# Retention of the first four heads moved beside the gate and query products of the last four

## The chip, the core and the metric

One core of a Trainium2 chip runs the whole program. The metric is the device time of one execution in microseconds (us); the median of three runs of the kernel before is 1373.83 us. All tensors in memory are float32. Where a product is written as three TensorE instructions (`mm3`), each factor has been split beforehand into a rounded part and a remainder of type fp32r ("high" and "low").

## What is computed

The reference is one layer of a hybrid network over 1024 tokens of width 1024, with 256 context tokens. Cut to what matters here:

```
hx  = modulate(rmsnorm(x), c);  ux = hx @ w_in            # 3584 columns
x0, x1, v = short_conv(ux[:, :1536])                      # three groups of 512
y_hy  = (long_conv(v * x1, filter) + bias * v * x1) * x0  # through a Fourier transform
q, k, v, g = ux[:, 1536:]                                 # 8 heads x 64 each
q, k  = rope(q), rope(k / 8)
o     = chunkwise retention forward + backward            # chunks of 128 tokens, state from context
y_ret = groupnorm(o) * gn * silu(g)
x     = x + gate1 * (concat(y_hy, y_ret) @ w_out)
x     = x + gate2 * (relu(modulate(rmsnorm(x)) @ w1)**2 @ w2);  out = rmsnorm(x)
```

`modulation()` makes the shift, scale and gate vectors: products of c with slices of w_ada, summed on VectorE (DVE).

## The kernel before, in words

The order in which work is traced gives each instruction a priority; a scheduler at build time then fixes one order for each engine by those priorities and its own estimate of when operands are ready. At run time each engine and each DMA queue goes through its list in order. `urgent()` raises the priority of what stands in it. The stages are:

1. Start (to about 54 us): norms, the filter network, the first two modulation vectors.
2. Key stage (54 to 260 us). The spectra of the filter are made (`pkf`), and for each half `hh` of the heads (four each) the keys (`pk`), values (`pv`) and their context forms (`pck`, `pcv`). Rotated keys `kr` (one buffer) are transposed (`pkT`) and weighted (`kw`, L779) for the chunk states (`pT`). The modulation vectors come in eight pieces of 512 columns. A piece is eight loads `adaw` (three buffers), eight DVE instructions into `adac` (L710, L712) and eight small matmuls `pada` (L715). Pieces 1 to 3 are traced in this stage, behind the value products.
3. Convolution (260 to about 520 us). For each half `hv` of the channels come the products x1, v and x0, features on partitions (`feature_major`: 96 matmuls of 512 columns for a slab of 256 features), the forward transforms `pXv`, the inverse `pGv`, butterflies on DVE, and a last multiplication by x0 (`vxl`) into `mix_d`. Pieces 4 and 5 of the modulation lie here.
4. Gates and queries (431 to 556 us), four slabs with tokens on partitions (`token_major`: 192 matmuls of 256 columns for a slab). Gates go through Silu; queries are rotated on DVE, written twice side by side (`q2`) and stored. Pieces 6 to 8 lie here.
5. Retention (556 to 672 us), 16 chunks, beside eight blocks `poh` of the output projection's convolution half (192 matmuls of 512 columns). A chunk loads its tiles, transposes the doubled queries (`pqd`), weights them (`qw`), copies them into zero-padded tiles (`sgqz`), forms the scores `psc` against the keys (two matmuls of 128 rows and 256 columns), masks them (`sT`) and forms `po` in 64-row halves.
6. The retention half of the projection (`por`), the second norm, and the two MLP products in Strassen form, to the end. Nothing here is changed.

A weight slab is loaded in two halves through one raw buffer `wr`, cast on ScalarE (ACT) and its remainder subtracted on DVE (`slab`, L205 to L207); two slabs are held at a time.

Of the kernel before, what the change touches and what calls it, by code (L numbers as in the profile page):

```python
# [17 lines left out]
P = 128  # L18
D = 1024
# [25 lines left out]
def shape_constants():  # L45
# [48 lines left out]
    rc = np.repeat(cs, 2, axis=1)  # L94
    rs = np.stack([-sn, sn], axis=-1).reshape(T, HD)
# [10 lines left out]
def lay_out(inputs):  # L106
# [3 lines left out]
    a = {n: k[n] for n in ("dft_f", "dft_i", "rope", "posd", "posr")}  # L110
# [20 lines left out]
    a["w_in"] = v["w_in"][0].reshape(KC, P, -1, 256).transpose(2, 1, 0, 3)  # L131
# [9 lines left out]
def tile_hymba_block(ctx: ExitStack, tc: tile.TileContext, I: dict, out: bass.AP, dbg=None, stop=99):  # L141
# [71 lines left out]
    for hv in range(2):  # L213
        cols += [("x1", hv, X1C + 256 * hv), ("vh", hv, VHC + 256 * hv), ("x0", hv, X0C + 256 * hv)]
    cols += [("g", 0, GC), ("g", 1, GC + 256), ("q", 0, QC), ("q", 1, QC + 256)]
# [350 lines left out]
    def rope(dst, ps, tab, n0, pool, nm, twice=None, tag="rope2", bufs=1):  # L566
# [4 lines left out]
        t2 = pool.tile([P, n, 256], F32, tag=tag, bufs=bufs, name=f"rp{nm}{n0}")  # L571
        for j in range(n):
            V.tensor_tensor(t2[:, j].rearrange("p (h i s) -> p h i s", h=4, s=2),
                            ps[:, j].rearrange("p (h i s) -> p h i s", h=4, s=2)[:, :, :, ::-1],
                            bc(tab[:, 1, n0 + j].rearrange("p (i s) -> p i s", s=2), 1, [P, 4, 32, 2]), op=ALU.mult)
        if twice is None:
            V.tensor_tensor(dst, dst, t2, op=ALU.add)
        else:
            V.tensor_tensor(twice, bc(dst.rearrange("p n (h d) -> p (n h) d", h=4), 2, [P, 4 * n, 2, HD]),
                            bc(t2.rearrange("p n (h d) -> p (n h) d", h=4), 2, [P, 4 * n, 2, HD]), op=ALU.add)  # L580
# [161 lines left out]
    for hh in range(2):  # L742
        hs = slice(4 * hh, 4 * hh + 4)
        kr = kvp.tile([P, NCH, 256], F32, tag="kr", name=f"kr{hh}")
# [55 lines left out]
        modulation()  # L800
        if hh == 1:
            modulation()
# [38 lines left out]
    for hv in range(2):  # L841
        vT = vtp.tile([P, NCH, 256], F32, tag="vT", name=f"vT{hv}")
        Gs = cvp.tile([P, 2, 8, 256], F32, tag="Gs", name=f"Gs{hv}")
# [6 lines left out]
        for b, ps in feature_major(("vh", hv), f"pvh{hv}"):  # L850
# [7 lines left out]
            for q in range(2):  # L858
# [3 lines left out]
                A.copy(vT[:, 4 * q:4 * q + 4, b * P:(b + 1) * P], pt.rearrange("p (c n) -> p c n", n=P))  # L862
        for b, ps in feature_major(("x0", hv), f"px0{hv}"):
# [4 lines left out]
            if b == 0:  # L868
                prefetch()
        modulation()  # L870
        prefetch()
        for r, u in butterflies(cvp, scp, vT, 256, f"v{hv}"):
# [88 lines left out]
        for ca, cb, ya, yb, sg in ((C16, S16, 1, 7, 1), (S16, C16, 3, 5, -1)):  # L961
# [7 lines left out]
            tt(Y[yb], z, sub, Y[yb])  # L969
        for b in range(2):  # L970
            blk = 2 * hv + b
            yv = yy[:, b].rearrange("p c n -> p (c n)")
            for q in range(2):
                cc = slice(q * 512, q * 512 + 512)
                vx = cvp.tile([P, 512], F32, tag="fx", bufs=2, name=f"vxl{blk}{q}")
# [7 lines left out]
                dbg(f"mix{blk}_{q}", vx)  # L983
    if stop <= 3:
        return


    sg_d = [tc.dram_tile([2, P, 1024], F32, name=f"sg_d{hh}") for hh in range(2)]
    q2_d = [tc.dram_tile([NCH, P, 8 * HD], F32, name=f"q2_d{hh}") for hh in range(2)]
    for hh in range(2):  # L990
        for g, ps in token_major(("g", hh), f"pgt{hh}"):
            sg = scp.tile([P, 4, 256], F32, tag="sc", bufs=3, name=f"sg{hh}{g}")
            with urgent():
                A.activation(sg, ps, AF.Silu)
                SP.dma_start(sg_d[hh][g], sg.rearrange("p n d -> p (n d)"))
            if hh + g < 2:
                modulation()
        prefetch()
    for hh in range(2):
        for g, ps in token_major(("q", hh), f"pq{hh}"):  # L1000
            with urgent():
                for m in range(2):
                    n0 = 4 * g + 2 * m

                    q2 = scp.tile([P, 2, 4, 2, HD], F32, tag="sc", bufs=3, name=f"q2{hh}{n0}")
                    qr = scp.tile([P, 2, 256], F32, tag="bfs", bufs=2, name=f"qr{hh}{n0}")
                    rope(qr, ps[:, 2 * m:2 * m + 2], ropes, n0, scp, f"q{hh}",
                         twice=q2.rearrange("p j h r d -> p (j h) r d"), tag="bfs", bufs=2)
                    SP.dma_start(q2_d[hh][n0:n0 + 2].rearrange("j p n -> p j n"),
                                 q2.rearrange("p j h r d -> p j (h r d)"))  # L1010
        if hh == 0:
            prefetch()
    cpool("cvp")
# [5 lines left out]

# [10 lines left out]
    rtl = opool("rtl", side="right")  # L1030
    rtp = opool("rtp", side="right")
# [3 lines left out]
    tabq = place(10, "tabq", F32)  # L1035
    SP.dma_start(tabq.rearrange("p a n -> p (a n)"), tab_d.rearrange("p a h n -> p (a h n)"))
    wqT, msk = [tabq[:, 2 * i:2 * i + 2].rearrange("p a (h n) -> p (a h) n", n=P) for i in range(2)]

    mx = [[place(2 * h + i, f"mx{h}{i}") for i in range(2)] for h in range(2)]
    ctrs = place(11, "ctrs", F32).rearrange("p a n -> p (a n)").rearrange("p (b j n) -> p b j n", b=2, j=4)  # L1040
    sgqz = place(12, "sgqz", F32)
    sg = sgqz[:, 0:2].rearrange("p a n -> p (a n)").rearrange("p (j n) -> p j n", j=4)
    mraw = place(13, "mraw", F32)


    qz = [sgqz[:, 2 + i].rearrange("p (h n) -> p h n", h=4) for i in range(2)]
    with urgent():
        for t in qz:
            V.memset(t, 0.0)
# [24 lines left out]
    def retention(hh, n, ctr, gss):  # L1074
        hs = slice(4 * hh, 4 * hh + 4)
        j = n % 4
        nm = f"{hh}_{n}"
        q2 = rtl.tile([P, 4, 2 * HD], F32, tag="q2", bufs=2, name=f"q2l{nm}")
        SP.dma_start(q2.rearrange("p h d -> p (h d)"), q2_d[hh][n])
        kt = rtl.tile([P, 2, P], F32, tag="ktl", bufs=2, name=f"ktl{nm}")  # L1080
        SP.dma_start(kt.rearrange("p a n -> p (a n)"), kT_d[hh][n])
        vt = rtl.tile([P, 256], F32, tag="vtl", bufs=2, name=f"vtl{nm}")
        SP.dma_start(vt, v_d[hh][n])
        st = rtl.tile([P, 256], F32, tag="stl", bufs=2, name=f"stl{nm}")
        SP.dma_start(st[0:64], st_d[hh][0, n])
        SP.dma_start(st[64:128], st_d[hh][1, 7 - n])
# [3 lines left out]
        pqv = pq.rearrange("p (h c) -> p h c", h=4)  # L1090
        qw = rtp.tile([P, 4, P], F32, tag="qw", bufs=2, name=f"qw{nm}")
        V.tensor_tensor(qw, pqv, wqT[:, hs], op=ALU.mult)
        qT = qz[n % 2]
        A.copy(qT[0:64, 0:4:2], pqv[0:64, 0:4:2])
        A.copy(qT[64:128, 1:4:2], pqv[64:128, 1:4:2])
        pc = ps_aux(f"psc{nm}")
        for pr in range(2):
            PE.matmul(pc[:, pr * 256:(pr + 1) * 256], lhsT=kt[:, pr],
                      rhs=qT[:, 2 * pr:2 * pr + 2].rearrange("p h c -> p (h c)"), start=True, stop=True)
        sT = rtp.tile([P, 4, P], F32, tag="sT", bufs=2, name=f"sT{nm}")  # L1100
        V.tensor_tensor(sT, pc.rearrange("p (h c) -> p h c", h=4), msk[:, hs], op=ALU.mult)
        po = ps_cv(f"po{nm}")
        for h in range(4):
            cc = slice(h * HD, (h + 1) * HD)
            for w, o, first in ((sT, vt, True), (qw, st, False)):
                for r in range(2):
                    rows = slice(64 * r, 64 * r + 64)
                    PE.matmul(po[rows, cc], lhsT=w[:, h, rows], rhs=o[:, cc], start=first, stop=not first)
        pov = po[:, 0:256].rearrange("p (h d) -> p h d", h=4)
        mu = rtp.tile([P, 4], F32, tag="mu", bufs=2, name=f"mu{nm}")  # L1110
        V.tensor_reduce(mu, pov, axis=AX.X, op=ALU.add)
        V.scalar_tensor_tensor(ctr[:, j].rearrange("p (h d) -> p h d", h=4), bc(mu, 2, [P, 4, HD]), -1.0 / HD, pov,
                               op0=ALU.mult, op1=ALU.add)
        sq = rtp.tile([P, 256], F32, tag="sqo", name=f"sqo{nm}")
# [482 lines left out]
```

## Time and profile before

| | |
|---|---|
| median of three runs | 1373.83 us (1373.09 to 1375.27) |
| profiled execution, its own time | 1370.97 us |
| span of its profile | 1369.2 us |
| TensorE (PE) matmuls busy | 1294.8 us, 95% of the span |
| DVE busy | 973.3 us, 71% |
| ACT busy | 533.6 us, 39% |
| mean granted TensorE clock | 0.980 |

The span is the time from the first to the last profiled instruction; the execution's own time is 1.8 us longer. A matmul's busy time overlaps its neighbours', so what a matmul costs is read from the distance between two starts.

### The profile page before, as it was taken

What the parts mean: (1) busy time and instruction counts of PE and PEld (TensorE: products, weight loads), DVE (VectorE), ACT (ScalarE), POOL (GpSimd) and SP (SyncE); (2) the same over time, 40 slices, a digit from 0 to 9 for tenths busy, and PEclk for the clock granted to TensorE, in tenths of its full rate; (3) what the DMA queues carried; (4) which work ended last, traced back from release to release, by engine and by line L of the source; (5) the groups of instructions that cost most, each with busy time, mean ns of one, the idle gap of its engine ahead of it and who ended that gap; (6) DMA issues with size and microseconds to landing.
All of it is one profiled execution on the core that took longest, in us unless ns stands there. A gap on an engine that the chain in (4) does not pass through costs nothing.

```text
span 1369.2 us, 20105 instructions
## 1 busy us (share of the span) xinstructions
PE 1294.8 (95%) x7386; PEld 1083.1 (79%) x7386; DVE 973.3 (71%) x1721; ACT 533.6 (39%) x912; POOL 19.4 (1%) x24
## 2 busy tenths in 40 slices
PE   6899899999999999799896999999998999999996
PEld 1479798988788999678776888888886888888896
DVE  5889787357878775558887988888656945555563
ACT  6863432213133121223455444444445744344420
POOL 0140000000000000000000000000000000000000
PEclk9799999999999999999998999999999999999999
DMA  9445766273536644776321789988636996666621
GB/s 374 175 151 160 233 206 212 79 228 129 169 120 215 206 162 155 270 243 182 104 96 64 251 306 326 348 302 300 238 123 232 338 321 190 193 201 185 199 79 62
DMA packets 139570, 278.19 MB, mean 203 GB/s; under 512 B 14672, under 2 KB 47056, under 8 KB 137040
## 3 DMA queue, kind: packets, MB, share of 16 engines
q1 hardware_dynamic: 137744, 272.19, 59.5%
q0 software_dynamic: 1152, 4.19, 0.8%
q8 instruction: 58, 0.95, 0.3%
q10 hardware_dynamic: 576, 0.52, 0.1%
q14 instruction: 40, 0.33, 0.1%
HBM read 193.75 MB, written 83.10 MB: 202 GB/s over the span
## 4 chain that ended last, share of the span: by engine, by line
PE 77%; DVE 8%; DMA 7%; ACT 4%; issue 2%; SPq 1%; POOL 0%; DVEq 0%; ACTq 0%; POOLq 0%
PE px L184 6%; PE px L185 6%; PE px L183 6%; PE pw L183 5%; PE py L183 5%; PE py L185 5%; PE py L184 5%; PE pw L185 5%; PE pw L184 5%; DMA dft_f_k<-in_dft_f 2%; PE pga L397 1%; PE pq L185 1%; PE pq L184 1%; PE pq L183 1%; PE pGv L901 1%
## 5 line engine op out<-in xcount | busy, mean ns | idle before, releaser
L1191 DVE TENSOR_TENSOR mt<-tr,mt 128x512 fp32r<-128x512 f32 x112 | 76.6, 688 | 99.6 <-ACT mt L1190 99.4
L1190 ACT CAST mt<-tr 128x512 fp32r<-128x512 f32 x112 | 69.6, 621 | 123.5 <-PE py L185 67.1
L183 PE MATMUL px<-mt,mw 128*128 128x512 f32 (+1 forms) x320 | 112.5, 352 | 3.0 <-ACT mw L1190 2.4
L184 PE MATMUL px<-mt,mw 128*128 128x512 f32 (+1 forms) x320 | 112.5, 352 | 0.7 <-DVE mt L1191 0.7
L185 PE MATMUL px<-mt,mw 128*128 128x512 f32 (+1 forms) x320 | 111.6, 350 | 0.0
L1191 DVE TENSOR_TENSOR mw<-wr,mw 128x512 fp32r<-128x512 f32 x112 | 76.6, 686 | 4.8 <-ACT mw L1190 4.4
L183 PE MATMUL py<-mt,mw 128*128 128x512 f32 x192 | 74.7, 389 | 0.0
L184 PE MATMUL py<-mt,mw 128*128 128x512 f32 x192 | 74.7, 389 | 0.0
L185 PE MATMUL py<-mt,mw 128*128 128x512 f32 x192 | 74.7, 389 | 0.0
L1190 ACT CAST mw<-wr 128x512 fp32r<-128x512 f32 x112 | 69.0, 617 | 9.8 <-DMA wr<-in_w_mlp 5.5
L183 PEld LDWEIGHTS px<-mt,mw 128*128 128x128 f32 x320 | 61.1, 191 | 11.4 <-ACT mw L1190 2.8
L184 PEld LDWEIGHTS px<-mt,mw 128*128 128x128 f32 x320 | 61.1, 191 | 9.2 <-DVE mt L1191 1.2
L185 PEld LDWEIGHTS px<-mt,mw 128*128 128x128 f32 x320 | 60.9, 191 | 8.2 <-DVE mw L1191 0.3
L183 PE MATMUL px<-hxh,wh_x 128*128 128x512 f32 x128 | 50.7, 396 | 0.0
L184 PE MATMUL px<-hxl,wh_x 128*128 128x512 f32 x128 | 50.6, 395 | 0.0
L185 PE MATMUL px<-hxh,wl_x 128*128 128x512 f32 x128 | 50.6, 395 | 0.0
L712 DVE SCALAR_TENSOR_TENSOR adac<-adaw,cs,adac 128x512 f32<-128x512 f32 x56 | 42.9, 766 | 9.8 <-DMA adaw<-in_w_ada 9.2
L185 PE MATMUL pk<-wh_k,hxl 128*128 128x256 f32 x128 | 39.2, 307 | 3.3 <-DVE hxl L438 3.3
L184 PEld LDWEIGHTS py<-mt,mw 128*128 128x128 f32 x192 | 36.0, 188 | 7.5
L183 PEld LDWEIGHTS py<-mt,mw 128*128 128x128 f32 x192 | 36.0, 188 | 7.5
L185 PEld LDWEIGHTS py<-mt,mw 128*128 128x128 f32 x192 | 36.0, 188 | 7.4
L183 PE MATMUL pk<-wh_k,hxh 128*128 128x256 f32 x128 | 39.6, 310 | 0.4 <-ACT hxh L434 0.4
(500 smaller groups left out, 3764.0 us busy)
## 6 DMA issues: line engine op xcount, KB each, us to landing
tr<-t_d SPq DMA_DIRECT2D x112, 256.0 KB, 4.0
adaw<-in_w_ada SPq DMA_DIRECT2D x64, 256.0 KB, 4.0
WH<-in_w_mlp SPq DMA_DIRECT2D x16, 1024.0 KB, 7.4
s_d<-WH SPq DMA_DIRECT2D x16, 1024.0 KB, 5.0
wr<-s_d SPq DMA_DIRECT2D x64, 256.0 KB, 4.0
wr<-in_w_mlp SPq DMA_DIRECT2D x48, 256.0 KB, 4.2
t_d<-c SPq DMA_DIRECT2D x40, 256.0 KB, 4.1
t_d<-CH SPq DMA_DIRECT2D x40, 256.0 KB, 5.4
```

What stands on the lines that cost most here:

```text
L183: PE.matmul(o, lhsT=lh, rhs=rh, start=first, stop=False, **kw)
L184: PE.matmul(o, lhsT=lh, rhs=rl, start=False, stop=False, **kw)
L185: PE.matmul(o, lhsT=ll, rhs=rh, start=False, stop=last, **kw)
L397: PE.matmul(pga[h][0:4, n, :], lhsT=cv[:, k, :], rhs=w_[:, n * 512:(n + 1) * 512], start=(k == 0), stop=(k == KC - 1 and i == 1))
L712: V.scalar_tensor_tensor(ac, wa, cs[:, k, 0:1], ac, op0=ALU.mult, op1=ALU.add)
L901: PE.matmul(o, lhsT=y[:, 0, cb], rhs=iv[:, sl[0]], start=True, stop=False)
L1190: A.copy(hi, src)
L1191: V.tensor_tensor(lo, src, hi.bitcast(F32), op=ALU.subtract)
```

## The change

Gates and queries become feature-major like the convolution's products. The columns of q and k in w_in are permuted on the host, so that the two members of a rotated pair lie 32 apart. The queries' partners are fetched by four transfers of 32 partitions within SBUF and multiplied with a table `ropeT` (`rot`). A chunk loads its queries already transposed, twice (64 partitions each), so that `pqd`, the doubled store and the zero-padded copies go. The scores become four matmuls of 64 rows and 128 columns, alternating between the lower and the upper 64 partitions, into two PSUM tiles. The retention of heads 0 to 3 runs in memory that the convolution leaves, beside the products of q and g of heads 4 to 7 (`gate_query(1)`); heads 4 to 7 run beside all eight blocks `poh`. Gated results of the first heads go through DRAM (`y_d`). The x0 slabs follow both halves' x1 and v. All eight modulation pieces are traced ahead of the key products, four for each half. From the seventh slab on, raw weights are loaded from POOL's queue.

```diff
@@ slab
-            SP.dma_start(raw, src[:, ks])
+            (SP if nxt[0] < 6 else G).dma_start(raw, src[:, ks])
@@ key stage
     for hh in range(2):
+        for _ in range(4):
+            modulation()
         kr = kvp.tile([P, NCH, 256], F32, tag="kr", name=f"kr{hh}")
...
         prefetch()
-        modulation()
-        if hh == 1:
-            modulation()
@@ convolution
-                vx = cvp.tile([P, 512], F32, tag="fx", bufs=2, name=f"vxl{blk}{q}")
+                vx = cvp.tile([P, 512], F32, tag="bfy", bufs=2, name=f"vxl{blk}{q}")
...
+    yy0 = conv_dft(0, conv_in(0))
+    vT1 = conv_in(1)
+    conv_gate(0)
+    with urgent():
+        conv_out(0, yy0)
+    conv_gate(1)
+    yy1 = conv_dft(1, vT1)
+    with urgent():
+        conv_out(1, yy1)
@@ gates and queries
-        for g, ps in token_major(("g", hh), f"pgt{hh}"):
...
-        for g, ps in token_major(("q", hh), f"pq{hh}"):
...
+    def gate_query(hh):
+        for b, ps in feature_major(("q", hh), f"pq{hh}"):
             with urgent():
+                qf = scp.tile([P, T], F32, tag="sc", bufs=3, name=f"qf{hh}{b}")
+                A.copy(qf, ps)
+                qs = scp.tile([P, T], F32, tag="sc", bufs=3, name=f"qs{hh}{b}")
+                for i in range(4):
+                    SP.dma_start(qs[32 * i:32 * i + 32], qf[32 * (i ^ 1):32 * (i ^ 1) + 32])
+                V.tensor_tensor(qs, qs, rot[:, 1], op=ALU.mult)
+                V.tensor_tensor(qf, qf, rot[:, 0], op=ALU.mult)
+                V.tensor_tensor(qf, qf, qs, op=ALU.add)
+                SP.dma_start(q_d[hh][b * P:(b + 1) * P], qf)
+            yield
+        prefetch()
+        for b, ps in feature_major(("g", hh), f"pgt{hh}"):
+            with urgent():
+                sg = scp.tile([P, T], F32, tag="sc", bufs=3, name=f"sg{hh}{b}")
                 A.activation(sg, ps, AF.Silu)
+                SP.dma_start(sg_d[2 * hh + b], sg)
+            yield
         prefetch()
+    for _ in gate_query(0):
+        pass
@@ retention
-        q2 = rtl.tile([P, 4, 2 * HD], F32, tag="q2", bufs=2, name=f"q2l{nm}")
-        SP.dma_start(q2.rearrange("p h d -> p (h d)"), q2_d[hh][n])
+        q2 = rtl.tile([P, 4, P], F32, tag="q2", bufs=2, name=f"q2l{nm}")
+        for r in range(2):
+            SP.dma_start(q2[64 * r:64 * r + 64], q_d[hh].rearrange("(h d) t -> d h t", h=4)[:, :, n * P:(n + 1) * P])
...
-        pq = ps_aux(f"pqd{nm}")
-        for h in range(4):
-            PE.transpose(pq[:, h * P:(h + 1) * P], q2[:, h], ident)
...
+        pc = [ps_aux(f"psc{nm}{s}") for s in range(2)]
         for pr in range(2):
-            PE.matmul(pc[:, pr * 256:(pr + 1) * 256], lhsT=kt[:, pr],
-                      rhs=qT[:, 2 * pr:2 * pr + 2].rearrange("p h c -> p (h c)"), start=True, stop=True)
+            for s in range(2):
+                rows = slice(64 * s, 64 * s + 64)
+                PE.matmul(pc[s][:, pr * P:(pr + 1) * P], lhsT=kt[rows, pr], rhs=q2[rows, 2 * pr + s],
+                          start=True, stop=True)
...
+    opool("gap", side="right").tile([P, 4 * 1024], F32, name="gap")
+    open_retention()
+    retention_tables(lambda nm: rt["l" if nm == "tabq" else "p"].tile([P, 4, 512], F32, name=f"{nm}0"))
+    products = gate_query(1)
+    def last_heads(g, j):
+        if j % 2:
+            next(products)
...
+    heads(0, last_heads)
+    cpool("rtp")
...
+    def projection(g, j):
+        if j % 2:
+            out_conv(4 * g + 2 * (j // 2))
+            out_conv(4 * g + 2 * (j // 2) + 1)
...
+        if (g, j) in ((0, 2), (1, 0)):
+            for i in range(2):
+                raw = mraw[:, 2 * (j // 2) + i]
+                SP.dma_start(raw, y_d[i][g])
+                split_ret(g, i, raw)
+    wo = []
+    heads(1, projection)
```

## Rows read from the trace of the kernel before

**Rows 1.** Stretch, length, busy us (count) of PE, PEld, DVE, ACT, POOL; clock; DMA.
```profile
54.00:205.00 151.00, 139.04 (x1022) 123.07 (x1022) 126.82 (x300) 74.17 (x148) 16.32 (x16) 0.95 0.60 188
205.00:240.00 35.00, 31.78 (x274) 29.30 (x273) 27.48 (x53) 9.94 (x21) 0.00 (x0) 1.00 0.71 212
240.00:260.00 20.00, 20.00 (x200) 18.68 (x200) 1.29 (x2) 4.31 (x11) 0.00 (x0) 1.00 0.10 36
260.00:555.60 295.60, 290.11 (x1695) 257.60 (x1693) 214.14 (x396) 65.07 (x87) 0.00 (x0) 1.00 0.53 175
555.60:570.00 14.40, 7.08 (x20) 4.77 (x19) 10.06 (x16) 4.52 (x7) 0.00 (x0) 0.76 0.68 219
570.00:672.00 102.00, 98.54 (x896) 77.85 (x897) 73.97 (x135) 32.28 (x71) 0.00 (x0) 1.00 0.63 203
```

**Rows 2.** Timeline of PE (start, us, engine, line): value products of the convolution, first and last of a stretch.
```profile
284.30 0.39 PE L183 MATMUL pvh<-hxh,wh_vh 128*128 128x512 f32 x1
...
297.90 0.39 PE L183 MATMUL pvh<-hxh,wh_vh 128*128 128x512 f32 x1
```

**Rows 3.** The query products' tile: count, shortest/median/longest ns, first and last start.
```profile
L183 PE MATMUL pq<-wh_q,hxh x128: 283/283/283, 509.4 to 555.1; 128*128 128x256 f32 x128
```

**Rows 4.** Timeline of PE in the retention stage: a group of each kind and its neighbours.
```profile
626.95 1.03 PE L1098 MATMUL psc<-sgqz,ktl 128*128 128x256 f32 x4
627.82 0.60 PE L1089 MATMUL pqd<-cols,q2l 128*128 128x128 f32 x4
628.17 0.48 PE L185 MATMUL poh<-mx,wl_o 128*128 128x512 f32 x1
628.49 0.39 PE L183 MATMUL poh<-mx,wh_o 128*128 128x512 f32 x1
628.81 0.34 PE L1108 MATMUL po<-vtl,sT 128*64 128x64 f32 x4
...
629.89 0.50 PE L184 MATMUL poh<-mx,wh_o 128*128 128x512 f32 x1
```

**Rows 5.** Timeline of all engines at the handover from queries to projection; brackets: idle before.
```profile
557.28 0.50 PE L183 MATMUL poh<-mx,wh_o 128*128 128x512 f32 x1 [1.66 <-ACT mx L1057]
...
560.53 0.59 PE L183 MATMUL poh<-mx,wh_o 128*128 128x512 f32 x1 [2.74 <-DVE rpq L573]
...
563.30 0.79 PE L184 MATMUL poh<-mx,wh_o 128*128 128x512 f32 x1 [2.19 <-DVE mx L1058]
```

**Rows 6.** Waits from 260 to 672 us: who waited for whom, us, times, longest.
```profile
PE pada L715 <- DVE adac L712: 2.0, 2, 1.1
PE pqd L1089 <- DMA q2l<-q_d: 1.7, 1, 1.7
PE psc L1098 <- ACT sgqz L1095: 1.6, 2, 0.9
```

**Rows 7.** DVE instructions by line and form: busy us, mean ns, idle before.
```profile
L712 DVE SCALAR_TENSOR_TENSOR adac<-adaw,cs,adac 128x512 f32<-128x512 f32 x56 | 42.9, 766 | 9.8 <-DMA adaw<-in_w_ada 9.2
L579 DVE TENSOR_TENSOR q<-qr,rpq 128x1024 f32<-128x1024 f32 x8 | 9.7, 1215 | 0.2
L573 DVE TENSOR_TENSOR rpq<-pq,ropes 128x256 f32<-128x256 f32 x16 | 6.0, 413 | 0.0
```

**Rows 8.** DVE's time in the modulation sums, key stage and behind it.
```profile
54.00:260.00 206.00, 12.40 (x16) 0.96 0.57 177
260.00:509.00 249.00, 34.29 (x48) 1.00 0.54 173
```

**Rows 9.** DMA issues by line: count, KB, median us to landing.
```profile
eo_d<-eo POOLq DMA_DIRECT2D x8, 512.0 KB, 4.4
wr_g<-in_w_in SPq DMA_DIRECT2D x4, 512.0 KB, 4.7
```

**Rows 10.** SP's queue: the second half's last two stores of the convolution's result.
```profile
514.28 0.32 SPq L982 DMA_DIRECT2D mix_d<-vxl  x1
...
522.01 0.32 SPq L982 DMA_DIRECT2D mix_d<-vxl  x1
```

More of the change, by code (lines that the diff above doesn't have):

```diff
@@ L129, in lay_out @@
     a["w_ada"] = v["w_ada"][0]
-    a["w_in"] = v["w_in"][0].reshape(KC, P, -1, 256).transpose(2, 1, 0, 3)
+    w = v["w_in"][0].copy()
+    for c0 in (QC, KCOL):
+        w[:, c0:c0 + 512] = w[:, c0:c0 + 512].reshape(D, NH, 32, 2).transpose(0, 1, 3, 2).reshape(D, 512)
+    a["w_in"] = w.reshape(KC, P, -1, 256).transpose(2, 1, 0, 3)
     a["w_out"] = v["w_out"][0].reshape(2, 4, P, 2, 512).transpose(0, 3, 2, 1, 4).reshape(4, P, 4, 512)
@@ L839, in short_conv, with conv_in @@
                                op0=ALU.mult, op1=ALU.add)
-    for hv in range(2):
+    def conv_in(hv):
         vT = vtp.tile([P, NCH, 256], F32, tag="vT", name=f"vT{hv}")
-        Gs = cvp.tile([P, 2, 8, 256], F32, tag="Gs", name=f"Gs{hv}")
         x1t = []
@@ L1013, in tile_hymba_block, with open_retention, retention_tables @@
-    cpool("cvp")
+    for _ in gate_query(0):
+        pass
+    rt = {}
+    def open_retention():
+        rt["l"] = opool("rtl", side="right")
+        rt["p"] = opool("rtp", side="right")
+    def retention_tables(new):
+        ctrs, sgs, tabq = [new(nm) for nm in ("ctrs", "sgs", "tabq")]
+        SP.dma_start(tabq.rearrange("p a n -> p (a n)"), tab_d.rearrange("p a h n -> p (a h n)"))
+        rt["wqT"], rt["msk"] = [tabq[:, 2 * i:2 * i + 2].rearrange("p a (h n) -> p (a h) n", n=P) for i in range(2)]
+        rt["ctr"] = ctrs.rearrange("p a n -> p (a n)").rearrange("p (b j n) -> p b j n", b=2, j=4)
+        rt["sg"] = sgs
@@ new lines, in group_norm @@
+    def group_norm(hh, g, sg, ctr, gss):
+        rtp = rt["p"]
+        gv = gss.rearrange("p n h -> p (n h)")
+        V.tensor_scalar(gv, gv, 1.0 / HD, EPS, op0=ALU.mult, op1=ALU.add)
+        rso = rtp.tile([P, 16], F32, tag="rso", bufs=2, name=f"rso{hh}{g}")
+        rsqrt_small(rso, gv, 16, rtp, f"o{hh}{g}")
+        zv = ctr.rearrange("p n (h d) -> p (n h) d", h=4)
+        V.tensor_tensor(zv, zv, bc(rso, 2, [P, 16, HD]), op=ALU.mult)
+        for pr in range(2):
+            pt = ps_cv(f"pz{hh}{g}{pr}")
+            for j in range(4):
+                PE.transpose(pt[:, j * P:(j + 1) * P], ctr[:, j, pr * P:(pr + 1) * P], ident)
+            blk = 2 * hh + pr
+            gn = colsA[:, GN + blk:GN + blk + 1]
+            V.scalar_tensor_tensor(sg[:, pr], pt, gn, sg[:, pr], op0=ALU.mult, op1=ALU.mult)
+            if hh == 0:
+                SP.dma_start(y_d[pr][g], sg[:, pr])
+            else:
+                split_ret(g, blk, sg[:, pr])
@@ new lines, in heads @@
+    def heads(hh, more):
+        pending = None
+        for g in range(2):
+            ctr = rt["ctr"][:, g]
+            gss = rt["p"].tile([P, 4, 4], F32, tag="gss", bufs=2, name=f"gss{hh}{g}")
+            for j in range(4):
+                retention(hh, 4 * g + j, ctr, gss)
+                if j == 1 and pending:
+                    group_norm(*pending)
+                if j == 1:
+                    sg = rt["sg"][:, 2 * g:2 * g + 2]
+                    for pr in range(2):
+                        SP.dma_start(sg[:, pr], sg_d[2 * hh + pr][:, 512 * g:512 * g + 512])
+                more(g, j)
+            pending = hh, g, sg, ctr, gss
+        group_norm(*pending)
@@ L1014, in tile_hymba_block @@
+    opool("gap", side="right").tile([P, 4 * 1024], F32, name="gap")
[5 more added lines that the diff above has]
+            next(products)
+        if (g, j) == (1, 3):
+            next(products, None)
+    heads(0, last_heads)
+    cpool("rtp")
+    cpool("rtl")
+    cpool("gap")
     cpool("vtp")
@@ L1072, in out_conv @@
             slabs.pop(("o", d // 4))
[L1074 to L1077, printed above, removed]
-        q2 = rtl.tile([P, 4, 2 * HD], F32, tag="q2", bufs=2, name=f"q2l{nm}")
-        SP.dma_start(q2.rearrange("p h d -> p (h d)"), q2_d[hh][n])
[L1080 to L1086, printed above, removed]
-        pq = ps_aux(f"pqd{nm}")
-        for h in range(4):
-            PE.transpose(pq[:, h * P:(h + 1) * P], q2[:, h], ident)
[L1090 to L1097, printed above, removed]
-            PE.matmul(pc[:, pr * 256:(pr + 1) * 256], lhsT=kt[:, pr],
-                      rhs=qT[:, 2 * pr:2 * pr + 2].rearrange("p h c -> p (h c)"), start=True, stop=True)
[L1100 to L1114, printed above, removed]
-        A.activation(sq, ctr[:, j], AF.Square)
-        V.tensor_reduce(gss[:, j], sq.rearrange("p (h d) -> p h d", h=4), axis=AX.X, op=ALU.add)
@@ L1164, in tile_hymba_block @@
-    group_norm(*pending)
+    for d in range(KC):
+        SP.dma_start(xn[d], I["xT"][d * P:(d + 1) * P])
+    def projection(g, j):
+        if j % 2:
+            out_conv(4 * g + 2 * (j // 2))
+            out_conv(4 * g + 2 * (j // 2) + 1)
+        if (g, j) == (0, 1):
+            wo.append(slab(I["w_out"][2], "o2", o2))
+        if (g, j) == (0, 3):
+            wo.append(wpool.tile([P, 4, 512], F32, tag="wh", bufs=2, name="o3r"))
+            SP.dma_start(wo[1], I["w_out"][3])
+        if (g, j) in ((0, 2), (1, 0)):
[3 more added lines that the diff above has]
+                split_ret(g, i, raw)
@@ L1165, in tile_hymba_block @@
+    wo = []
+    heads(1, projection)
+    o3r = wo.pop()
     with urgent():
```

159 lines of the change are left out of this document (69 added, 90 removed).

## Prediction

> **What bounds the kernel now.** I read the busy time by stretch first. From 260 to 555.6 us PE is busy 290.1 of 295.6 us and from 570 to 672 us 98.5 of 102, while DVE has 214.1 and 74.0 [rows 1]. The reader should see that TensorE's own work sets the time of the convolution, of the gate and query products and of the retention. A reordering there gains nothing by itself: it must remove PE work or PE's holes. Three places differ. In the key stage PE lacks 15.2 us (139.0, 31.8 and 20.0 of 206) and DVE is busy 155.6 us; 18.7 of its 50.4 idle us lie in the last 20 us, where PE is full [rows 1]. Second, the 14.4 us from 555.6 hold 20 matmuls and a clock of 0.76 [rows 1]. Third, the retention pays for small fp32 matmuls between the large ones.
>
> Since busy times overlap, I took prices from the distance of starts in PE's timeline. The convolution's products start 60 matmuls in 297.90 - 284.30 = 13.60 us, 0.227 us each for 512 columns [rows 2]. Query products start 127 triples in 45.7 us, 0.120 us each for 256 columns [rows 3]. Then I read the handover, the waits and the lines of DVE [rows 5 to 8].
>
> The sum is made against the profiled execution, 1370.97 us (span 1369.2 and 1.8 around it). The median of the runs shown, 1373.83, is 2.9 us above it; I add the sum's difference to the median. A difference under 0.2%, 2.7 us, can hardly be told from none.
>
> **1. Gates and queries feature-major.** A slab is 192 x 0.120 = 23.0 us now and 96 x 0.227 = 21.8 after [rows 2, 3]. Four slabs: -5.0 us, within half a microsecond, as both forms run in this trace. The queries' rotation becomes three DVE passes of 1024 columns for each of four half slabs, about 1.2 us a pass (the form of L579 [rows 7]), 15 us in all, behind an ACT copy and a transfer of partners. It is hidden by the next half slab's 48 x 0.227 = 10.9 us, as PSUM holds two. Uncovered, it would cost the last block's chain once, some 10 us, but the last blocks are gates, which need one ACT pass.
>
> **2. Transposes of the queries go.** Four `pqd` take 628.17 - 627.82 = 0.35 to 0.36 us, 16 chunks: -5.8 us [rows 4]. ACT's zero-padded copies go too; they ended two holes of PE, 1.6 us [rows 6], counted in 5.
>
> **3. Scores.** Four instructions of 256 columns take 627.82 - 626.95 = 0.87 us [rows 4]. After there are eight of 128 columns (two passes for each of four matmuls), on alternating halves of the rows. The trace shows no pairs of row halves. Upper bound: each costs half of one now, 0.11 us, plus 0.1 us at both ends, as a large matmul beside a `po` group takes 0.32 instead of 0.227 us [rows 4]: 1.08 us, +3.4 us for 16 chunks. Lower bound: they overlap as the `po` groups do, which use column halves: 32 of 64 columns in 629.89 - 628.81 = 1.08 us, 0.034 each [rows 4]; at 128 columns 0.067, 0.54 us a chunk, -5.3 us. `po` is the nearest kin, so I take its rate with both ends paid, 0.74 us: -2 us.
>
> The boundary of 0.1 us above is a row. The Trainium skill (TensorEngine Tiling (Array Packing), Key Properties) has a rule on each side: tiles of a split array work in parallel, and a change of the tiling mode drains the engine. By the first alone the scores would save 0.43 us a chunk, about 7 us; by the drain without overlap they would lose the 3.4 us. No trace so far shows such pairs of row halves.
>
> **4. The handover.** In the 14.4 us behind the last query product, 20 matmuls at 0.227 need 4.5 us: 9.9 us are lost, through a cast (1.66), DVE's rotation of the last queries (2.74), the remainder of the mixed block (2.19) and the low clock, 0.76, after those holes [rows 1, 5]. After, the same handover stands behind the last gate product, since the split convolution result still takes the memory of `hx`. DVE's rotation is gone from it, and raw blocks can be loaded ahead. I take half, -5 us; bounds 0 and, if only the first cast is left, -8.2.
>
> **5. Other holes from 260 to 672 us.** PE lacks 5.5 us up to 555.6 and 3.5 after 570 [rows 1]; the waits on `pada`, on the queries' load and on the copies are 5.3 of them [rows 6]. I take -2.5; bounds 0 and -5.3. The first heads' retention needs PE about 8 x 1.8 us plus transposes, 16 us, beside two slabs, 43.5 us; the second heads the same beside 192 x 0.227 = 43.6. Each chunk has four small DVE passes and one more of 0.41 us (the mask in two halves, L573's form [rows 7]); DVE has 28 us free there [rows 1]. So retention lies beside other work as before, and only its place changes.
>
> **6. Modulation in the key stage.** Of 64 sums, 46.7 us, 16 run there now; 48 more are 34.3 us for DVE [rows 8]. Its queue would be busy 189.9 of 206 us. Behind an `adac` stand the rotation of the keys, `kw` and the transforms' sums; PE waits for those. What hides them is DVE's idle time, 50.4 us, and that PE has the next products. Lower bound nothing: the weights `kw` are late by less than the 21.8 us of the next slab. Upper bound: the 18.7 us at the end help nobody, the idle rest is used only to half, so 34.3 - 16 = 18 us reach PE, and six more `pada` groups wait 1.1 us each as the longest now [rows 6]: 25 us. Where 48 sums lie today, PE waited 2.0 us on them [rows 6], with DVE idle 28% of the time against 24% in the key stage [rows 1]; I take +4, nearer to that row. Their loads matter less: DVE idled 9.2 us on them in the whole run [rows 7].
>
> **7. Edits costed at nothing.** Twenty-two half slabs move to POOL's queue. A store there lands in 4.4 us, a slab half on SP's in 4.7 [rows 9]; two halves with a cast and a remainder of some 1.2 us each (L579's form) take 14 us of a slab's 21.8, so 7 us more would be needed before PE sees it. SP gains free slots and gives them to 16 partner transfers, one more query load a chunk and four `y_d` stores. The x0 slabs only change places among equal matmuls. `vx` in its own buffers shortens the last multiplication, whose stores are now 7.7 us apart [rows 10].
>
> Sum: -5.0 - 5.8 - 2 - 5 - 2.5 + 4 = -16.3 us, 1354.7 for the profiled execution and 1357.5 for the median. All bounds low: -5 - 5.8 - 5.3 - 8.2 - 5.3 = -29.6, 1344. All high: -5 - 5.8 + 3.4 + 25 = +17.6, 1391.
>
> **The rivals.**
> *A. DVE becomes the bound of the key stage (slower).* Place: 54 to 240 us, where DVE already has 154.3 of 186 us [rows 1]. For it: 34 us are put where 31.7 are idle, and `kr` has one buffer, so the second half's rotation waits for the first half's `kw`. Against it: PE can take the values' or x1's products meanwhile. Price: term 6 at its upper bound, -20.3 + 25 = +4.7, 1378.5. It decides from 23 us on.
> *B. The cover comes late.* The first heads' memory is free only when the second half's convolution has stored its result. Now that is 33 us before the last query product [rows 3, 10], so of the x0 slab and four others behind the second value slab, 21.8 + 92 = 114 us, some 80 pass beside it; after there are two x0, a q and a g slab, 87 us: a margin of 7 us. If it is 20 us late, PE takes the last heads' products ahead, a retention without cover idles about half of that, and the handover keeps its price: -16.3 + 10 + 5, near 1372.5. Against it: three pieces of modulation leave DVE's queue there, and the stores come closer together.
> *C. Row halves don't overlap.* The scores cost +3.4 instead of -2: 1363. [...]
> *D. Nothing is lost.* Terms 3 to 5 near their low bounds and term 6 near nothing: 1346.
>
> **How the numbers follow.** Forecast (1351 to 1361): 0.42. C (1361 to 1366): 0.13. B (1366 to 1376.5): 0.15. A (above 1376.5): 0.17. D (below 1351): 0.13. Time 1358, that of the likeliest. The range from 1346 to 1379 leaves out the lower half of D and two thirds of A, under 0.2; the likeliest case's own range is 1351 to 1361. Faster by over 0.2% is below 1371.1: forecast, C, D and a little under half of B, 0.74. Same, 1371.1 to 1376.6: 0.09. Slower: A, 0.17.
>
> **What would show it.** Right: gate and query matmuls of 512 columns start 0.227 us apart; no `pqd`; PE fuller than 95% from the first gate product to `por`; `por` begins some 15 to 20 us earlier, the later stages moved but not changed. Term 6: PE's idle time from 54 us to the first x1 product against 15.2 us, and DVE's share there. Term 3: time from a score group's first start to the next group. Term 4: idle and clock behind the last gate product. The prediction is wrong if PE's idle time in the key stage grows by 20 us, if PE shows a stretch of score and `po` groups with holes and no products beside them, or if a slab's cast waits on POOL's loads while PE is idle.

## The result, and the profile after

The changed kernel takes 1449.35 us (median of 4 runs, 1447.31 to 1451.6), the kernel before 1374.55 in the same session: a ratio of 1.0535, interval 1.0499 to 1.0572. It is 75 us slower. The forecast was 1358, the range ended at 1379; the prediction was wrong in sign and in size. The profiled execution took 1449.73 us, its span is 1448.0.

The busy time by stretch comes first again (columns as in [rows 1]).

```profile
54.00:125.00 71.00, 65.07 (x435) 57.24 (x436) 63.23 (x142) 41.79 (x74) 16.05 (x15) 0.91 0.44 144
125.00:205.00 80.00, 39.59 (x144) 28.18 (x143) 57.28 (x134) 16.09 (x42) 0.00 (x0) 0.73 0.71 216
205.00:250.00 45.00, 25.85 (x147) 20.75 (x145) 22.48 (x43) 7.74 (x17) 0.00 (x0) 0.75 0.56 173
250.00:345.00 95.00, 87.94 (x822) 82.39 (x822) 45.99 (x93) 21.46 (x42) 0.00 (x0) 0.95 0.41 131
345.00:641.00 296.00, 293.17 (x1495) 239.19 (x1493) 197.24 (x368) 71.88 (x97) 10.11 (x19) 1.00 0.50 157
641.00:681.00 40.00, 15.04 (x118) 11.26 (x116) 20.56 (x38) 12.46 (x17) 1.58 (x3) 0.57 0.87 294
681.00:741.00 60.00, 60.00 (x510) 46.85 (x507) 38.68 (x77) 9.97 (x21) 0.00 (x0) 1.00 0.52 153
```

Two stretches stand out. From 125 to 250 us PE is busy 65.4 of 125 us at a clock of about 0.74, and DVE is idle 45.2 of those us: the key stage, which ended near 260 us, ends at 345. And from 641 to 681 PE has 15.0 of 40 us at 0.57: the handover. To set the two kernels side by side, the span is cut at four starts on PE's timeline: the last context product of the values (pcv), the last of the gate and query products, the first por, the first pw of the stage behind it. The table has the distances in us, for the kernels of the experiments as well (e1, e5, e8 and e9, told of below):

| stretch ending with | before | after | e1 | e5 | e8 | e9 |
|---|---|---|---|---|---|---|
| last pcv (from 0) | 259.4 | 345.4 | 266.2 | 269.4 | 263.8 | 265.6 |
| last gate or query product | 296.0 | 295.5 | 308.7 | 311.7 | 293.0 | 296.8 |
| first por | 99.7 | 100.3 | 97.9 | 80.1 | 87.3 | 92.9 |
| first pw behind por | 60.3 | 49.9 | 49.9 | 54.2 | 60.5 | 51.7 |
| end of the span | 653.9 | 656.9 | 656.8 | 654.9 | 655.7 | 654.9 |

After against before: +86.0, -0.5, +0.6, -10.4 and +3.0, together +78.8 before rounding, the difference of the two spans. So the loss is all in the key stage, and the rest gained 7 us where 20 were forecast. No edit is aimed at the last row, and it still differs by 3 us; a difference of that size between two traces says little.

**The key stage.** PE's timeline has the fourth modulation piece, the first key transposes and the first context product behind each other:

```profile
225.43 1.87 PE L718 MATMUL pada<-ones,adac 128*128 128x2 f32 x8 [5.41 <-DVE adac L715]
227.16 2.89 PE L761 MATMUL pkT<-cols,kr 128*128 128x128 f32 x12
233.57 0.79 PE L761 MATMUL pkT<-cols,kr 128*128 128x128 f32 x4 [3.52 <-ACT kt L764]
238.00 0.58 PE L188 MATMUL pck<-wh_k,hch 128*128 128x256 f32 x1 [3.64 <-ACT kt L764]
...
247.86 0.39 PE L188 MATMUL pk<-wh_k,hxh 128*128 128x256 f32 x1 [0.52 <-ACT wh_k L211]
```

The first keys' products had ended at 101 us, and DVE had written the last of the rotated keys (kr) at 107. Their transposes come 120 us later, at 227.2, right behind the fourth pada. ACT's timeline names what waits next, the cast of the second keys' slab:

```profile
246.76 1.04 ACT L211 CAST wh_k<-wr_k 128x1024 fp32r<-128x1024 f32 x1 [4.64 <-PE pck L190]
```

The reader is to see a chain, not a busy engine. The slabs have two buffers, those of the first keys and values. The keys' is held until pck has read it; pck stands behind pkT, and pkT behind pada. So from 132 us, where the values' products end, to 238 PE has only the filter transforms and the pada groups, and the second keys' products start at 247.9. The profile puts PE's long stops in between (9.2, 7.7 and 7.9 us) down to an operand of the transforms, urk; the reader is to ask not only what a stop waits for but which products should have filled it. In the second half the transposes come right behind the eighth pada too (314.7), but from 265 to 315 us PE has the second keys' and values' products and is busy 47.9 of 50 us: there the order costs little.

**The handover.** PE's timeline behind the last gate product, which starts at 640.91, only the lines with a wait of over 2 us:

```profile
646.23 0.34 PE L1091 MATMUL po<-vtl,sT 128*64 128x64 f32 x4 [3.01 <-DVE sT L1083]
652.04 0.48 PE L1091 MATMUL po<-vtl,sT 128*64 128x64 f32 x4 [2.31 <-DMA vtl<-v_d]
659.40 1.94 PE L1113 MATMUL pz<-cols,ctrs 128*128 128x128 f32 x8 [5.28 <-DVE ctrs L1109]
675.54 0.79 PE L188 MATMUL poh<-mx,wh_o 128*128 128x512 f32 x1 [14.20 <-ACT mx L1187]
```

SP's queue in the same stretch:

```profile
649.25 5.23 SPq L1212 DMA_DIRECT2D XN<-in_xT  x7
661.31 1.18 SPq L1118 DMA_DIRECT2D y_d<-sgs  x2
662.54 0.46 SPq L1212 DMA_DIRECT2D XN<-in_xT  x1
663.04 0.77 SPq L1064 DMA_DIRECT2D q2l<-q_d  x1
663.86 0.60 SPq L1051 DMA_DIRECT2D tabq<-tab_d  x1
664.56 3.34 SPq L1185 DMA_DIRECT2D mraw<-mix_d  x4
```

The last two chunks of the first heads run with no product beside them, and the raw blocks of the convolution (mraw), traced ahead of XN's loads, go out behind them and behind the last y_d stores: the first poh comes 34.6 us after the last gate product. Before, it came 2.2 us after the start of the last triple of query products [rows 3, 5].

### The profile page after: what moved, and what is told of

The parts are those of the page before. It is cut to its first block, busy times and chain, and to the rows that moved or that the text cites. A ratio compares the mean times of both kernels' runs of the same rounds, so it can differ in the third digit from the quotient of the medians.

```text
span 1448.0 us, 19385 instructions
## 1 busy us (share of the span) xinstructions
PE 1305.2 (90%) x7002; PEld 1066.0 (74%) x7002; DVE 973.0 (67%) x1719; ACT 529.3 (37%) x886; POOL 31.2 (2%) x46
## 4 chain that ended last, share of the span: by engine, by line
PE 71%; DMA 12%; DVE 9%; ACT 4%; issue 3%; SPq 1%; POOL 1%; ACTq 0%; DVEq 0%; POOLq 0%
PE px L188 5%; PE px L190 5%; PE px L189 5%; PE py L188 5%; PE py L190 5%; PE py L189 5%; PE pw L188 5%; PE pw L190 5%; PE pw L189 5%; DMA dft_f_k<-in_dft_f 2%; DMA adaw<-in_w_ada 1%; PE po L1091 1%; PE pga L404 1%; PE poh L190 1%; PE poh L188 1%
```

## The experiments

**Where the 75 us are: the PSUM pair of pada.** e1 is the changed kernel with

```
-        pt = ps_aux(f"pada{i}")
+        pt = ps_cv(f"pada{i}")
```

> The changed kernel, with one edit: the PSUM tile of a modulation piece (pada) comes from the pair of buffers that the filter transforms use, no longer from the pair of the key transposes (pkT), the context products (pck), the state products (pT) and the score products. Theory P (turn of PSUM buffers): pkT and pck of the first keys were allotted their buffers behind four pada tiles, so they could not start before the fourth piece was summed (225 us after the start), and with them the slab of the first keys stayed held and the second keys' products had no weights. Then the key stage ends near 265 to 275 us instead of 345, and the whole comes to 1365 to 1385 us. Theory D (DVE is the bound: 48 more sums): the sums still take DVE and all behind it waits as before; 1430 us or more. Theory L (the 64 loads of 256 KB delay the other loads on SP's queue): also 1430 us or more.

e2 has the eight `modulation()` calls of the changed kernel at the old places, PSUM as it was.

> The changed kernel with the eight modulation pieces back at their places in the kernel before (one behind the first values, two behind the second, one behind each half's gates of the convolution, three between the query and gate products). It measures the rest of the change alone. By the trace of the changed kernel the distance from the first x1 product to the first retention product of the output was 395.7 us against 392.1 before, so the rest gave nothing: 1370 to 1382 us. By the prediction's terms 1 to 5 (-20.3 us) it should be 1354; if moving the modulation away from the convolution had been a gain in itself, the loss shows as more than 1382.

e3 is the kernel before with its modulation calls moved, e4 the same with the line of e1:

```
     for hh in range(2):
         hs = slice(4 * hh, 4 * hh + 4)
+        for _ in range(4):
+            modulation()
...
-        modulation()
-        if hh == 1:
-            modulation()
...
-        modulation()
...
-            if hh + g < 2:
-                modulation()
```

> The kernel before with one edit: its eight modulation pieces stand in the key stage, four ahead of each half's key products, as in the changed kernel. Theory P: the whole loss comes from there, 1374 + 75 to 85, so 1445 to 1460 us. If the loss needs other parts of the change as well (the order of the slabs, the POOL queue, the layout of the keys), 1375 to 1400 us.

> The run before this one (modulation early in the kernel before), with pada in the filter transforms' pair of PSUM buffers. Theory P: the loss goes, 1370 to 1390 us, and what stays over 1374 is what the 48 sums and their loads cost DVE and the queue by themselves (the prediction had +4 with bounds 0 and +25). Theories D and L: as without the edit, 1430 us or more.

Measured: e1 1381.7 us (ratio to before 1.0036, 1.0013 to 1.0058), e2 1380.6 (1.0016, 0.9997 to 1.0036), e3 1444.7 (1.0484, 1.0436 to 1.0532), e4 1377.2 (0.9992, 0.9973 to 1.0012). Theory P stands, and from both sides: the move alone costs the kernel before 67 of the 75 us (e3), and one other pair of PSUM buffers takes 68 us off either kernel (1449.4 to 1381.7, 1444.7 to 1377.2). With the pieces at the old places the loss is gone as well (e2). The tile view of pkT and of pada in e1 (count, shortest, median and longest ns, first and last start):

```profile
L761 PE MATMUL pkT<-cols,kr x32: 271/272/329, 110.1 to 216.0; 128*128 128x128 f32 x32
...
L718 PE MATMUL pada<-ones,adac x64: 165/251/272, 229.2 to 335.2; 128*128 128x2 f32 x64
```

The stretch from 54 to 260 us, first of the changed kernel:

```profile
54.00:260.00 206.00, 139.88 (x857) 114.29 (x858) 147.32 (x322) 71.99 (x147) 16.05 (x15) 0.81 0.57 179
```

and then of e1:

```profile
54.00:260.00 206.00, 187.79 (x1453) 168.14 (x1454) 162.69 (x365) 85.70 (x173) 16.02 (x15) 0.95 0.58 185
```

With the other pair pkT starts at 110 us instead of 227. In those 206 us DVE does more than in the changed kernel (162.7 against 147.3 us), not less, and PE has 188 us of work instead of 140. In e4 it is the same: 162.4 and 187.3 us, pkT from 110.6. So theory D, DVE as the bound, falls.

The one line also moves the pieces, and that limits what e1 and e4 show. In the pair of the filter transforms a pada comes behind these transforms: the first runs at 229 us, and five of the eight pieces lie in the convolution. The modulation sums and their pada in the same stretch (PE, PEld and DVE alone), the changed kernel and then e1:

```profile
54.00:260.00 206.00, 4.82 (x32) 4.78 (x32) 29.65 (x40) 0.81 0.57 179
...
54.00:260.00 206.00, 3.02 (x24) 2.99 (x24) 20.18 (x27) 0.95 0.58 185
```

By 260 us 40 of the 64 sums have run in the changed kernel, 27 in e1 and in e4, 16 in the kernel before. Two things are therefore not separated. The early sums and their loads (theory L) may lengthen the chain by setting the pace of the four pieces: DVE waits 11 us for adaw between 125 and 250 us. And a part of the wait may be pkT's place in PE's list and not the buffer: DVE had read the third piece's result at 211.5, which by turns of two frees a buffer, and pkT still comes behind the fourth pada.

**Where the rest of the gain went: the handover.** The changed kernel with the modulation at its old places (e2) takes the time of the kernel before (+3 us, the interval holds 1), where terms 1 to 5 of the prediction summed to -20.3. e1 still has the hole (last gate product 574.9, first poh 607.2). Two causes were open, the memory of the raw blocks and their place in SP's queue. The 14 places after the handover were one pool, whose memory lies partly on the first heads' retention. e5 gives mraw and mx a pool of their own, opened ahead, in the memory of the normed input:

```
+    own = opool("own")
...
+    mraw = place(13, "mraw", F32)
+    mx = [[place(2 * h + i, f"mx{h}{i}") for i in range(2)] for h in range(2)]
     xnp = opool("xnp")
...
-    big = opool("big")
+    rt["big"] = opool("big")
```

> The run with pada in the other PSUM pair, and one more edit: the five 8 KB places of the convolution's raw and split result (mraw, mx) become a pool of their own in the memory of the normed input, opened ahead of the XN buffers, and the other places follow behind XN. Theory H (handover): the rest of the change loses its gains in the 32 us behind the last gate product (575 to 607 us in that run: 9.2 us of products, clock 0.60), because one pool of 14 places lies partly on the first heads' retention buffers and all of it waits for their last y_d store (595 us). Freed of that, the raw blocks are loaded right behind the last gate product, the first poh starts near 580 to 585 us instead of 607, and the whole comes to 1350 to 1362 us (1381.7 - 22 to 30). Theory R (the last chunks of the first heads' retention are the wait, whatever is loaded): 1375 or more. If the gain is smaller than 10 us, a part of the hole lies elsewhere.

e6 opens `xnp` ahead of `own` and has XN's loads ahead of the raw blocks' in the program.

> As the run before it, but the XN buffers and their eight loads of 512 KB stand ahead of the raw blocks, in memory and in order, so that SP's queue holds the raw blocks behind XN's loads and behind the last y_d stores again. It tells which of the two made the hole. Theory H (memory alone): the raw blocks may be loaded at the last gate product, at the cost of XN's 4 MB in front: some 10 us more than the run before, 1362 to 1370 us. Theory Q (the place in SP's queue decides too): the raw blocks come again only behind the y_d stores at about 595 us, and the time stays at that of the run with the common pool, 1375 to 1385 us.

e7 is e2 with the own pool.

> The changed kernel with modulation at its old places (PSUM pair as it was) and the own pool for the convolution's raw and split result. 1380.6 without the own pool. Theory H: 1350 to 1362 us, as the run with modulation in the key stage and the other PSUM pair, since moving 48 sums by itself was worth nothing within 3 us. If modulation in the key stage helps once the convolution and the handover are free of holes, this run is slower than that one by 3 us or more; if it costs DVE there, faster.

e8 is e5 with `SP.dma_start` for all slabs.

> The run with the own pool, with all weight slabs loaded from SP's queue again, none from POOL's. The prediction put the POOL queue at nothing. Theory N (nothing hangs on the queue): within 3 us of the run with the own pool. Theory S (SP's queue is crowded where the convolution, the partner transfers and the retention loads meet): 5 us or more slower. If a slab from POOL's queue waits for the remainder before it (0.53 us of issue, in order behind DVE), the run is faster.

Measured: e5 1370.8 us (0.9962, 0.994 to 0.9984), e6 1381.9 (1.0055, 1.0036 to 1.0074), e7 1367.3 (0.9938, 0.9912 to 0.9963), e8 1367.3 (0.9939, 0.9922 to 0.9956). The own pool gave 11 us, not the 22 to 30 expected. In e6 the memory is free by the layout, and still the raw blocks went out at 595.9 us, behind the last y_d stores at 594.1; the time is that of e1. So theory H was half the cause: memory and queue each hold the raw blocks. Free memory with the old place in the queue gives nothing (e6), with a place ahead of XN's loads about half (e5). e8 shows what is left. SP's queue:

```profile
574.22 0.33 SPq L1118 DMA_DIRECT2D y_d<-sgs  x1
...
577.13 0.40 SPq L1068 DMA_DIRECT2D vtl<-v_d  x1
577.62 0.47 SPq L1070 DMA_DIRECT2D stl<-st_d  x1
578.14 0.59 SPq L1071 DMA_DIRECT2D stl<-st_d  x1
578.78 2.00 SPq L1185 DMA_DIRECT2D mraw<-mix_d  x4
```

and PE, the last gate product and the first poh:

```profile
556.75 0.40 PE L190 MATMUL pgt<-hxh,wl_g 128*128 128x512 f32 x1
...
584.17 1.22 PE L188 MATMUL poh<-mx,wh_o 128*128 128x512 f32 x2
```

The memory is free when the last gate product ends, at 557 us; the loads stand 22 us longer in SP's queue, behind the loads of the last chunks and the first two y_d stores. The longest wait of that queue there is such a store: 3.9 us, for DVE's part of the group norm, until 574.2. Whether POOL's queue for the slabs costs by itself stays open: e5 and e8 differ by 3.5 us, and their intervals overlap. The table's second row is 13 to 16 us longer in e1 and e5 than in the changed kernel, and not in e8 and e9, which have the slabs on SP's queue but also three retention chunks fewer in that row; what of it is the queue is not separated. The same holds for the place of modulation, e5 against e7.

e9 is e8 with the raw blocks and XN on POOL's queue, e10 is e7 with the same two lines and all slabs on SP's queue, e11 is e9 with the two score loops exchanged:

```
-            SP.dma_start(raw, mix_d[k][:, cc])
+            G.dma_start(raw, mix_d[k][:, cc])
...
-        SP.dma_start(xn[d], I["xT"][d * P:(d + 1) * P])
+        G.dma_start(xn[d], I["xT"][d * P:(d + 1) * P])
```
```
-        for pr in range(2):
-            for s in range(2):
+        for s in range(2):
+            for pr in range(2):
```

> The run with the own pool and all slabs on SP's queue (1367.3 us), with the eight loads of the convolution's raw blocks and XN's eight loads issued from POOL's queue, which then has nothing else. In that run the last gate product ended at 557 us, the memory of the raw blocks was free at once, and yet their loads went out only at 578.8 us, because SP's queue held them behind the loads of the last retention chunk, which wait for a buffer; the first poh came at 584 us. Theory Q (the place in SP's queue is what is left of the handover): the first poh comes within 8 us of the last gate product, lies beside the last chunks of the first heads, and the time falls by 12 to 20 us, to 1347 to 1355. Theory R (retention of the first heads is the chain: it starts when the second half's convolution is stored and takes 5 to 6 us a chunk whatever runs beside it): poh comes early but the second heads' retention starts no earlier, por waits for it, and the time falls by less than 6 us.

> The same with the modulation pieces at their old places and pada in its old PSUM pair: the rest of the change with every wait found so far taken out, and the convolution with 56 pada matmuls' worth of modulation beside it again. Theory: within 4 us of the run with modulation in the key stage; the prediction's terms 1 to 5 (-20.3 us) would put it at 1354 or a little above. Slower by 5 us or more would mean that moving the modulation is a gain once its PSUM buffers are out of the way.

> The run with the raw blocks on POOL's queue, with the four score matmuls of a chunk in another order: both of the upper 64 rows first, then both of the lower, where the changed kernel alternates. One look, for the length of a score group. If the two row halves work at the same time only when they alternate, a group of eight (two passes for each of four) takes about 0.9 us from its first start to the next group instead of 0.65; if the order is of no account, 0.65 again; by the rule that a change of tiling drains the engine, the alternating order would be the longer one, and this one shorter than 0.65.

Measured: e9 1364.6 us (0.9915, 0.9897 to 0.9934), e10 1366.4 (0.9923, 0.9904 to 0.9943), e11 one run of 1361.7. In e9 the raw blocks leave POOL's queue at 546.4 us, while the last slab is multiplied, and PE has

```profile
562.39 0.40 PE L190 MATMUL pgt<-hxh,wl_g 128*128 128x512 f32 x1
...
567.66 0.79 PE L188 MATMUL poh<-mx,wh_o 128*128 128x512 f32 x1
...
591.00 1.23 PE L1079 MATMUL psc<-q2l,ktl 64*128 64x128 f32 x8 [7.31 <-DMA ktl<-kT_d]
```

The first poh comes 5.3 us after the last gate product, as theory Q has it, but the time fell by only some 3 us (the intervals of e8 and e9 overlap), as theory R has it: PE now stands 7.3 us for keys. The score groups are in the order of the chunks, eight chunks to each half of the heads, and this is the seventh: the keys are those of the first heads' seventh chunk, not of the second heads. Their load meets XN's 4 MB; e12 puts the second half of XN into memory that becomes free later (two pools, `xnp0` and `xnp1`, with `big` between them).

> The run with the raw blocks and XN on POOL's queue (1364.6 us), with the second half of XN (2 MB of 4) in memory that the first heads' retention frees, so that its loads go out behind the last chunks. In that run PE stood 7.3 us at 583.7 us for the keys of the second heads (ktl), whose loads met XN's 4 MB (the transfers were busy all of 570 to 584 us), and ran at half clock behind it. Theory T (traffic: XN's loads delay the loads of the second heads): the wait shrinks below 3 us and the time falls by 5 to 9 us, to about 1357. Theory F (SP's queue, first in first out, holds ktl behind a buffer's wait): the wait stays, and so does the time within 3 us.

Measured: 1364.9 us (0.9906, 0.9873 to 0.994), the same. The wait for ktl shrank to 0.5 us, as theory T has it, but not the time: the gain went into the next wait, at the first po of the second heads:

```profile
616.77 0.48 PE L1091 MATMUL po<-vtl,sT 128*64 128x64 f32 x4 [4.64 <-issue]
```

DVE had waited for the second heads' tables, which lie in the common pool and left SP's queue only at 610.1 us:

```profile
615.64 0.69 DVE L1073 TENSOR_TENSOR qw<-q2l,tabq 128x512 f32<-128x512 f32 x1 [0.96 <-DMA tabq<-tab_d]
```

e9 and e12 beat both kernels: 11 to 13 us, 0.9%, under the kernel before and some 84 under the changed one.

## Why the prediction was wrong

**Term 6, the step that failed.** It priced the moved modulation by DVE's time and by pada's own wait ("six more `pada` groups wait 1.1 us each as the longest now"), +4 with bounds 0 and +25. Shown: the key stage lost 86 us, and 68 us of the time go with one pair of buffers. What the term left out is what a waiting pada holds: a PSUM buffer out of the pair that pkT, pck and pT use, given out in the order of the program. At the old places one piece stood in front of the second key transposes (pada at 186.7, pkT at 193.9), and none in front of the first. Ahead of the key products, four pieces come before the first key transpose, and the last of them is summed at 225 us. The price is that chain's: four pieces, then the transposes, pck, the slab. The prediction did ask who waits for pada and answered with DVE's queue; the buffer's queue was not looked at. Its price for DVE is not shown wrong: in e4, where the sums spread to 335 us, the whole time is that of the kernel before (0.9992), and what 48 sums more by 260 us would cost without the buffer's chain no run shows.

One of the prediction's signs of being wrong, 20 us more idle time of PE in the key stage, came out: by the first four rows above PE lacks 72.5 us from 54 to 345 us, where it lacked 15.2.

**Rival A** named the right place and the right sign, by the wrong mechanism: DVE is idle 45 us of the 125 in which PE starves, and its upper price, +25, is a third of what the stage lost.

The Trainium skill has the sign of this (Perfetto Trace Analysis, Optimization Strategy): the same gap repeated on an engine that should be full can mean that there is no PSUM or SBUF for the next tile. The trace agrees: the three stops of 7.7 to 9.2 us between 125 and 250 us are such a gap, put down to urk, and in e1, with another buffer for pada, no wait for urk of over 0.6 us is left from 54 to 250 us.

**Terms 1 and 2 held.** Gate and query matmuls of 512 columns start 0.23 us apart (640.44, 640.67, 640.91), and there is no pqd any more, as [rows 2, 4] had it. The stretch up to the last gate product is as long as before (295.5 against 296.0 us) although 6 of the 16 retention chunks now lie in it; the seven pada groups that lay there before are gone from it.

**Term 3 held, from other parts.** A score group of the changed kernel with its neighbours, and what stood in front of the group of [rows 4] in the kernel before:

```profile
636.81 0.40 PE L189 MATMUL pgt<-hxl,wh_g 128*128 128x512 f32 x1
637.14 0.71 PE L1079 MATMUL psc<-q2l,ktl 64*128 64x128 f32 x8
637.78 0.50 PE L190 MATMUL pgt<-hxh,wl_g 128*128 128x512 f32 x1
638.12 0.40 PE L188 MATMUL pgt<-hxh,wh_g 128*128 128x512 f32 x1
...
626.72 0.40 PE L184 MATMUL poh<-mx,wh_o 128*128 128x512 f32 x1
626.95 1.03 PE L1098 MATMUL psc<-sgqz,ktl 128*128 128x256 f32 x4
```

The group takes 0.64 us to the next start, against 0.87 [rows 4]. The large matmul in front of it takes 0.33 us where it took 0.23; the one behind takes 0.1 us more in both kernels. So where a large matmul stands in front a chunk costs 0.64 + 0.10 = 0.74 us, and 16 such chunks save 2 us, as summed, though a pass takes 0.08 us where 0.067 stood and only one of the two ends that were paid is new. In e11, whose order keeps the halves apart:

```profile
533.92 0.72 PE L1079 MATMUL psc<-q2l,ktl 64*128 64x128 f32 x8
534.58 0.50 PE L189 MATMUL pgt<-hxl,wh_g 128*128 128x512 f32 x1
```

With 0.66 us the order of the halves is of no account, and rival C falls. The two rules of the Trainium skill (TensorEngine Tiling (Array Packing), Key Properties) are both compatible with it: split tiles run in parallel, and the drain stands there for a change of the tiling mode and not of the tile alone, so it says nothing against alternating halves. The trace bounds it: a drain can be no more than the 0.1 us that large matmuls take longer, once at each end.

**Term 4 failed at its argument.** "Raw blocks can be loaded ahead" was the reason for -5; the layout and SP's queue load them last, and the handover grew from 14.4 us with 7.1 of matmuls [rows 1] to 40 with 15.0. Term 5 held up to there (PE lacks 2.8 of 296 us from 345 to 641, where it lacked 5.5), but its sentence that retention lies beside other work as before did not. Rival B is borne out in part: the first heads' first score group came at 603.3 us, 38 us before the last gate product, so two of eight chunks had no cover. The prediction gave B a margin of 7 us and 15 in 100.

**What came back unforeseen** is the 10.4 us between por and the stage behind it. In the kernel before, the last chunks ran into por (until 671.4, with por from 655.1); after, retention is done when por starts. That is why all behind the key stage came out 7 us shorter in spite of the hole.

With pada's pair, the pool and the queue mended (e9), the change gives -11 us, two thirds of the -16.3 summed for it. Where the other third is, the runs show in part: each mended wait uncovered another, shorter one (ktl, then tabq), and the key stage of e9 is 6.3 us longer than before. They come with the moved pieces, since e4, which moves nothing else, has its last pcv at 265.7 too; by which wait was not settled. e10, with the pieces at their old places and the key stage as before (last pcv at 259.0), is no faster on the whole: -9.3 us, where terms 1 to 5 summed to -20.3.

## What to carry to other kernels

Before moving work that is small on its engine, list every resource that its instructions hold while they wait: the PSUM buffer, the SBUF buffer, the place in each DMA queue. Then ask what the program hands the same resource to next; if that feeds the bounding engine, the price is the whole chain and not the waiting time seen at the old place. Where several things hold one transfer (memory and queue, here), undo them together before judging, since one alone may show nothing.

## What the runs showed of the hardware

PE's granted clock was 0.73 and 0.75 over 125 us in which it was half busy, for the most part with transforms of 256 columns, and 0.57 in the handover: the lower of its two levels (1.2 and 2.4 GHz) for half or more of those stretches, or for nearly all of the last one. A short wait can cost the full level as well: in e5, PE ran large matmuls without a gap, waited 2.9 us for a pada, ran its eight small matmuls, and the large matmuls behind them start 0.43 us apart until 326.1, where the next take 0.23. PE's timeline of e5:

```profile
319.26 1.73 PE L718 MATMUL pada<-ones,adac 128*128 128x2 f32 x8 [2.87 <-DVE adac L715]
320.85 0.77 PE L190 MATMUL pvh<-hxh,wl_vh 128*128 128x512 f32 x1
321.42 0.63 PE L188 MATMUL pvh<-hxh,wh_vh 128*128 128x512 f32 x1
...
326.11 0.47 PE L190 MATMUL pvh<-hxh,wl_vh 128*128 128x512 f32 x1
326.42 0.40 PE L188 MATMUL px<-hxh,wh_x 128*128 128x512 f32 x1
326.66 0.40 PE L189 MATMUL px<-hxl,wh_x 128*128 128x512 f32 x1
```

From 320.85 to 326.11 there are 12 steps, 5.26 us instead of 12 x 0.227 = 2.72: the low level adds 2.5 us to the wait's 2.9, so this wait cost nearly twice its length.
